# Merge gates of the tail in pairs by seven block products instead of eight

## The chip, the cores and the metric

The kernel runs on one core of a Trainium2 chip. The metric is device time in microseconds of one execution. The core's engines are named as in the profile: PE (matmuls), DVE, ACT and POOL (element-wise work), SP (issues the DMAs).

## The reference, cut to what matters

Two layers; in each, a combined projection of h = RMSNorm(x) gives the inputs of four branches A, B, C, M and the logits of four merge gates. Sequence length and model width are both 1024.

```python
h = rms_norm(x, norm_g)
z = h @ w_in                                   # a_u, a_v, a_gate, ..., merge_logits (4 x 1024 columns)
y_a = chunked_spatial_gating(gelu(a_u), gelu(a_v), ...) * silu(a_gate)
y_b, y_c, y_m = ...                            # attention, state space layer, memory attention
gates = sigmoid(merge_logits + b_merge).reshape(bsz, seq, 4, 1024)
merged = sum(gates[:, :, i] * (y_i @ w_br_i) for i in range(4))
x = x + merged @ w_out
```

The merge logits alone are a product of 1024 x 1024 by 1024 x 4096 in each layer.

## The kernel before, in words

Activations lie transposed: channels on the 128 partitions, 1024 tokens along the free dimension. x times its norm gain stands in eight tiles `xg[0..7]`, one for each 128 input channels. Every fp32 product is made of three matmuls: each operand is split into a rounded high part and the rest (`xh`, `xl`; `wh`, `wl`), and hi·hi, hi·lo and lo·hi are summed in PSUM (`mmr`, L176). The rest is one subtraction: by DVE, or by POOL when `split` or `wsplit` is told so (both under `tt`, L96). A cast of raw weights is DVE's (L152).

A block of 128 output channels (`cm`) is 48 matmuls of 512 columns: 8 input tiles x 3 products x 2 token halves. `cmn` adds the row scale: one DVE operation that reads PSUM and multiplies by `rsb`. A merge gate is such a block, then a tanh with the bias on ACT. There are 32 gates in a layer, index (i, c): branch i, 128-channel block c.

In each layer the work around the change runs in this order:

1. Attention, with fillers in the gaps of PE's queue (`background`): the silu gate blocks of branches B, C, M, whose results go to DRAM (`ysscr`), and 10 of the 32 merge gates (the list `BG`: all eight of i = 1, and (3, 6), (3, 7)), written to DRAM (`bgscr`).
2. `branch_a`: two products `av` (96 matmuls of 256 columns each), each followed by a chain on DVE, ACT and POOL (gelu, norm, split); then four blocks au0, ag0, au1, ag1 of 48 matmuls, each evicted from PSUM by DVE; then the spatial product (`pv`, 4 times 3 matmuls), transposes (`tr`) and the split results `yah`, `yal`.
3. `merge` for i = 0, 2, 3, 1. For each c: the gate, computed in place (48 matmuls, DVE, ACT) or fetched from `bgscr`; the product y_i @ w_br_i (12 matmuls, 24 for i = 1); the eviction `stt` on DVE, which multiplies by the gate; and an addition into `merged` (on POOL, on DVE for the last i). 22 gates of a layer are computed in place. `gated` fetches the split inputs of the next merge from `ysscr`, in the midst of the merge before it (`AH`).
4. Eight blocks of the output product and the residual.

The PSUM pool for blocks (`mm`) holds two tiles of 128 x 1024: the block after next has to wait for an eviction. A scheduler sets the order on each engine's queue from priorities in program order; each engine then takes its queue strictly in that order.

Of the kernel before, what the change touches and what calls it, by code (L numbers as in the profile page):

```python
# [44 lines left out]
class Trunk:  # L45
# [174 lines left out]
    def setup(self):  # L220
# [45 lines left out]
        self.bgscr = self.dp.tile([len(BG), P, S], F32, name="bgscr")  # L266
# [984 lines left out]
    def background(self, l, bi, bias=None, y=None, ri=None, dst=None):  # L1251
# [4 lines left out]
        low = lambda: self.tc.high_priority(offset=-LOW)  # L1256
        with self.tc.high_priority(offset=-800):
            hi, lo = self.wsplit(self.a["w_cm"][l, bi], 1024, bg=True)
# [66 lines left out]
    def branch_a(self, l):  # L1325
# [7 lines left out]
        for tg in range(2):  # L1333
            ps = self.mm()
            for j in range(4):
# [71 lines left out]
    def merge(self, l, i, ys, first=False, last=False, ahead=None):  # L1407
# [8 lines left out]
        res = None  # L1416
# [7 lines left out]
        for c in range(8):  # L1424
            if ahead and ahead[0] == c:
                res = ahead[1]()
# [23 lines left out]
        return res  # L1450

    def run(self):
# [17 lines left out]
        for l in range(self.L):  # L1470
# [72 lines left out]
AH = (6, 4, 3)  # L1543
# [123 lines left out]
```

## Time and profile before

| | us |
|---|---|
| median of 3 runs | 2438.87 (2436.58 to 2439.66) |
| the profiled execution, its own time | 2440.25 |
| its span in the profile | 2438.5 |
| PE busy | 2325.2 (95%) |
| DVE busy | 1215.9 (50%) |
| POOL busy | 775.0 (32%) |
| ACT busy | 706.5 (29%) |

Busy is the time in which an engine had an instruction in it, its waiting inside one included. Layer 1's branch A runs from 720.7 to 789.4 us, its merges from there to 1132 and its output product to 1236; in layer 2 branch A runs from 1920.5 to 1989.6 and the merges to 2332.

### The profile page before, as it was taken

To read this page: it belongs to the slowest core of one execution; us is meant where nothing else is said; L and a number is where in the kernel's file an instruction comes from. 1 tells how busy PE (TensorE), PEld (TensorE's weight loads), DVE (VectorE), ACT (ScalarE), POOL (GpSimd) and SP (SyncE) were. 2 spreads that over 40 slices of the span, in tenths; PEclk is the share of its full clock that TensorE was granted. 3 is DMA by queue.
4 is the path that set the end of the run, shared out by engine and by line. 5 is a ranking of instruction groups with operands and counts; after the bars stand their busy time and mean duration, and the time that the engine had idled before them with its cause. 6 is when DMAs were issued, how large, how long until landed. Compare 5 with 4: busy or idle time off the path is not lost. (4 is left out here: it accounts for less than half of the span.)

```text
span 2438.5 us, 28178 instructions
## 1 busy us (share of the span) xinstructions
PE 2325.2 (95%) x11174; PEld 1855.2 (76%) x11174; DVE 1215.9 (50%) x1871; ACT 706.5 (29%) x1233; POOL 775.0 (32%) x605
## 2 busy tenths in 40 slices
PE   7998889989999999999999888999999999999999
PEld 5766677867778888888877666787777888888887
DVE  6455784366676323236244556714666652233351
ACT  4121253247762101101111213522577420111010
POOL 3533113432304214342435421143322132244411
PEclk9999999999999999999999999999999999999999
DMA  4226343242332112222432363413423211122342
GB/s 153 75 93 184 115 138 102 82 123 79 95 106 66 61 44 70 69 77 105 156 100 73 96 188 108 139 49 103 125 83 109 80 44 52 56 92 79 103 156 69
DMA packets 91700, 237.56 MB, mean 97 GB/s; under 512 B 25200, under 2 KB 34352, under 8 KB 91568
## 3 DMA queue, kind: packets, MB, share of 16 engines
q1 hardware_dynamic: 91568, 235.76, 30.4%
q8 instruction: 88, 1.44, 0.2%
q14 instruction: 44, 0.36, 0.1%
HBM read 175.27 MB, written 60.46 MB: 97 GB/s over the span
## 5 line engine op out<-in xcount | busy, mean ns | idle before, releaser
L96 POOL TENSOR_TENSOR wl<-wr,wh 128x1024 fp32r<-128x1024 f32 (+3 forms) x125 | 295.9, 2367 | 946.1 <-DVE wh L152 634.7
L176 PE MATMUL mm<-xh,wh 128*128 128x512 f32 x1216 | 378.7, 392 | 9.1 <-ACT xh L106 8.7
L152 DVE CAST wh<-wr 128x1024 fp32r<-128x1024 f32 (+2 forms) x110 | 78.4, 713 | 618.6 <-PE mm L176 539.8
L176 PE MATMUL mm<-xh,wl 128*128 128x512 f32 x1216 | 376.1, 390 | 0.8 <-POOL wl L96 0.8
L176 PE MATMUL mm<-xl,wh 128*128 128x512 f32 x1216 | 376.8, 390 | 0.0
L176 PEld LDWEIGHTS mm<-xh,wh 128*128 128x128 f32 x1216 | 227.3, 188 | 59.9 <-ACT xh L106 8.7
L176 PEld LDWEIGHTS mm<-xh,wl 128*128 128x128 f32 x1216 | 228.3, 188 | 49.7 <-POOL wl L96 1.6
L176 PEld LDWEIGHTS mm<-xl,wh 128*128 128x128 f32 x1216 | 228.4, 188 | 49.0 <-issue 0.8
L176 PE MATMUL bg<-xh,bh 128*128 128x512 f32 x576 | 229.2, 416 | 15.5 <-DVE bgx L96 15.5
L176 PE MATMUL bg<-xl,bh 128*128 128x512 f32 x576 | 226.3, 411 | 0.0
L176 PE MATMUL bg<-xh,bl 128*128 128x512 f32 x576 | 224.1, 409 | 1.0 <-POOL bl L96 1.0
L96 POOL TENSOR_TENSOR bl<-br,bh 128x1024 fp32r<-128x1024 f32 x36 | 96.4, 2678 | 317.0 <-DVE bh L152 203.3
L106 ACT ACTIVATE cmn<-cmn,bmh 128x1024 f32<-128x1024 f32 x44 | 50.6, 1151 | 440.7 <-DVE cmn L96 440.7
L96 DVE TENSOR_TENSOR pT<-tr,pT 128x512 fp32r<-128x512 f32 x224 | 125.6, 571 | 42.8 <-ACT pT L106 42.1
L176 PEld LDWEIGHTS bg<-xh,bh 128*128 128x128 f32 x576 | 111.8, 195 | 46.0 <-DVE bgx L96 25.6
L176 PE MATMUL pv<-pT,v 128*128 128x512 f32 (+3 forms) x384 | 134.0, 388 | 7.9 <-DVE pT L96 5.1
L106 ACT ACTIVATE pT<-tr 128x512 fp32r<-128x512 f32 x224 | 111.0, 505 | 86.6 <-PE tr L1087 77.3
L176 PEld LDWEIGHTS bg<-xh,bl 128*128 128x128 f32 x576 | 111.1, 193 | 24.9 <-issue 3.2
L1054 DVE TENSOR_REDUCE mx<-mm 128x1 f32<-128x128 f32 (+7 forms) x128 | 96.5, 754 | 64.5 <-PE mm L176 63.7
L176 PEld LDWEIGHTS bg<-xl,bh 128*128 128x128 f32 x576 | 111.3, 194 | 21.8 <-issue 4.0
L106 ACT ACTIVATE pr<-mm,nm,qs 128x128 f32<-128x128 f32 (+7 forms) x128 | 106.3, 830 | 0.9
L1087 PE MATMUL tr<-ident,pr 128*128 128x128 f32 x576 | 97.9, 275 | 0.3 <-ACT pr L106 0.2
(449 smaller groups left out, 4173.7 us busy)
## 6 DMA issues: line engine op xcount, KB each, us to landing
wr<-in_w_cm_dram SPq DMA_DIRECT2D x76, 512.0 KB, 3.6
br<-in_w_cm_dram SPq DMA_DIRECT2D x36, 512.0 KB, 3.7
bgscr<-bgx SPq DMA_DIRECT2D x20, 512.0 KB, 3.1
gate<-bgscr SPq DMA_DIRECT2D x20, 512.0 KB, 5.6
ysscr<-bgx SPq DMA_DIRECT2D x16, 512.0 KB, 2.6
br<-ysscr SPq DMA_DIRECT2D x16, 512.0 KB, 3.4
wr<-in_w_out_dram SPq DMA_DIRECT2D x16, 512.0 KB, 3.7
bgr<-riscr SPq DMA_DIRECT2D x24, 256.0 KB, 4.8
```

The lines of the kernel that those rows point to most:

```text
L96: (eng or self.nc.vector).tensor_tensor(out=out, in0=x, in1=y, op=op)
L106: self.nc.scalar.activation(out, x, f, **k)
L152: self.nc.vector.tensor_copy(hi[:, :n], raw)
L176: self.nc.tensor.matmul(out, lhsT, rhs, start=start, stop=stop)
L1054: nc.vector.reduce_max(out=mx, in_=ps[:, 0:n], axis=AX.X)
L1087: nc.tensor.transpose(pt[:, k * P:(k + 1) * P], pts[k][:, st * P:(st + 1) * P], self.ident)
```

## The change

The 22 gates that were computed in the merges are computed ahead of them, as 11 pairs (c, c+1), and written to `bgscr` like the others; the merges fetch all 32.

A pair is a product of two 128-row weight blocks with x: seen as 2 x 2 blocks (output block by half of the input channels; half of the input channels by half of the tokens), it takes eight block products. Strassen's form (Winograd's variant) makes it of seven, with sums of the weight blocks and of the x blocks. A block product is 12 matmuls of 512 columns, so a pair is 84 matmuls instead of 96.

The sums of x are formed once in a layer from the split parts (`xh`, `xl`), for k = 0..3, and are split again: T3, T2 in `x_sums` (k = 0, 1 in program order behind the first av product's matmuls, k = 2, 3 behind the second's), T4 in `x_sums2` behind each au block, T1 in `x_sums3`, which overwrites the second token half of `xg[0..3]`. The weight sums are formed for each pair: four DVE additions and seven splits, each split a copy on ACT and a subtraction, two of them on DVE and five on POOL. A product's result is combined by DVE additions that read PSUM; the row scale becomes a POOL multiplication, then come tanh and DMA by halves of 512 columns.

```diff
+            for k in range(2):
+                self.x_sums(2 * tg + k)
...
+            for k in range(2):
+                self.x_sums2(2 * b + k)
...
+        self.x_sums3()
...
+    def x_sums(self, k):
...
+        self.tt(t3, h22, h12, SUB, eng=g)
+        self.tt(t2, l22, l12, SUB)
+        self.tt(t3, t3, t2, ADD)
+        self.split(*self.T[3][k], t3)
+        self.tt(t1, h12, h11, SUB, eng=g)
+        self.tt(t2, t3, h11, ADD)
+        self.tt(t2, t2, l11, ADD)
+        self.split(*self.T[2][k], t2)
+        self.tt(t3, l12, l11, SUB, eng=g)
+        self.tt(t1, t1, t3, ADD, eng=g)
+
+    def x_sums2(self, k):
...
+        self.tt(a, h21, h2, SUB, eng=self.nc.gpsimd)
+        self.tt(b, l21, l2, SUB)
+        self.tt(a, a, b, ADD)
+        self.split(*self.T[4][k], a)
+
+    def x_sums3(self):
+
+        for k in range(4):
+            self.split(*self.T[1][k], self.t1[k // 2][:, k % 2 * 512:k % 2 * 512 + 512])
+
+    def pair_weights(self, aps):
...
+        self.tt(s1, a21, a22, ADD)
+        self.tt(s2, s1, a11, SUB)
+        self.tt(s3, a11, a21, SUB)
+        self.tt(s4, a12, s2, SUB)
+        for i, a in enumerate((a11, s2, s3, a12, s1, a22, s4)):
+            w = self.U("sw", F32R)
+            hi, lo = half(w)
+            self.split(hi, lo, a, sub_eng=self.nc.vector if i in (1, 4) else self.nc.gpsimd)
+            yield hi, lo
...
+            def prod(ps, x):
+                hi, lo = ws[len(nws)]
+                for k in range(4):
+                    xh, xl = self.T[x][k]
+                    sl = slice(k * P, (k + 1) * P)
+                    self.mmr(ps, hi[:, sl], xh, k == 0, False)
+                    self.mmr(ps, hi[:, sl], xl, False, False)
+                    self.mmr(ps, lo[:, sl], xh, False, k == 3)
...
+            self.act(u1, prod(q1, 11), AF.Copy)
+            self.tt(u2, prod(q2, 2), u1, ADD)
+            q1, q2 = half(self.mm())
+            self.tt(u3, prod(q1, 3), u2, ADD)
+            finish(0, c1[0], prod(q2, 21), u1)
+            q1, q2 = half(self.mm())
+            p5 = prod(q1, 1)
+            self.tt(u4, p5, u2, ADD)
+            finish(1, c2[1], p5, u3)
+            finish(0, c2[0], prod(q2, 4), u3)
+            finish(1, c1[1], prod(self.pv(), 22), u4)
+            done(c1, c2)
...
+        def finish(h, out, x, y):
+            self.tt(out, x, y, ADD)
+            self.tt(out, out, self.rsb[:, h * 512:h * 512 + 512], MUL, eng=self.nc.gpsimd)
...
-            if (i, c) in BG:
-                g = self.U("gate")
-                nc.sync.dma_start(out=g, in_=self.bgscr[BG.index((i, c))])
-            else:
-                g = self.cmn(l, B_MRG + 8 * i + c)
-                self.act(g, g, AF.Tanh, scale=0.5, bias=self.bm_half[:, l * 32 + 8 * i + c:l * 32 + 8 * i + c + 1])
+            g = self.U("gate")
+            nc.sync.dma_start(out=g, in_=self.bgscr[8 * i + c])
...
-                self.tt(self.mg[c], self.mg[c], g, ADD, eng=None if last else nc.gpsimd)
+                self.tt(self.mg[c], self.mg[c], g, ADD, eng=nc.gpsimd if c % 2 and not last else None)
...
-            ys = self.merge(l, 0, ysa, first=True, ahead=(AH[0], lambda: self.gated(2, 2)))
-            ys = self.merge(l, 2, ys, ahead=(AH[1], lambda: self.gated(3, 0)))
-            ys = self.merge(l, 3, ys, ahead=(AH[2], lambda: self.gated(1, 4)))
-            self.merge(l, 1, ys, last=True)
+            self.gate_pairs(l, todo[::2], lambda: get(2, 0))
+            self.merge(l, 0, ysa, first=True, ahead={2: lambda: get(3, 0)})
+            self.merge(l, 2, ys[2], ahead={0: lambda: get(1, 4)})
+            self.merge(l, 3, ys[3])
+            self.merge(l, 1, ys[1], last=True)
```

Two smaller edits: the last filler gate of attention, (1, 3) of `bg_gate`, loses its low priority (`fore`), and `gated` takes its raw tiles from the general pool.

How the queues change is seen at three places of layer 1. The first is DVE at the second eviction of branch A, `av<-mm,rs` (the first av's chain ends with `av<-av,ry,ga x4`). Before:

```order
L103 SCALAR_TENSOR_TENSOR av_1279_6288<-av_1279_6288,ry_1283_6301,ga_1273_6185 128x256 x4
L96 TENSOR_TENSOR av_1287_6426<-mm_1286_6329,rs_63_381 128x1024
L100 TENSOR_SCALAR avt_1288_6427<-avt_1288_6427 128x1024
L96 TENSOR_TENSOR avt_1288_6427<-avt_1288_6427,av_1287_6426 128x1024
L103 SCALAR_TENSOR_TENSOR av_1287_6426<-avt_1288_6427,av_1287_6426 128x1024
```

After, with `tp` and `T` the tiles of the x sums:

```order
L103 SCALAR_TENSOR_TENSOR av_1291_6324<-av_1291_6324,ry_1295_6337,ga_1273_6185 128x256 x4
L96 TENSOR_TENSOR tp_1299_6462<-xl6_38_185,xl2_26_145 128x512
L96 TENSOR_TENSOR tp_1299_6462<-tp_1299_6462 128x512
L96 TENSOR_TENSOR tp_1300_6475<-xl7_41_195,xl3_29_155 128x512
L96 TENSOR_TENSOR tp_1299_6462<-tp_1299_6462,xh2_25_144 128x512
L96 TENSOR_TENSOR T_1286_6295<-tp_1299_6462,T_1284_6293 128x512
L96 TENSOR_TENSOR tp_1299_6462<-tp_1299_6462,xl2_26_145 128x512
L96 TENSOR_TENSOR tp_1300_6475<-tp_1300_6475 128x512
L96 TENSOR_TENSOR av_1301_6488<-mm_1298_6365,rs_63_381 128x1024
L96 TENSOR_TENSOR T_1282_6291<-tp_1299_6462,T_1280_6289 128x512
L96 TENSOR_TENSOR T_1286_6295<-tp_1300_6475,T_1284_6293 128x512
L96 TENSOR_TENSOR tp_1300_6475<-tp_1300_6475,xh3_28_154 128x512
```

Seven operations of `x_sums` now stand between the end of the first chain and that eviction, and more of them between the steps of the second chain behind it.

The second is PE at the end of branch A (`pv` the spatial product, `tr` its transposes, `mm_1341` the first merge gate before; `mm_1371` with weight `sw` the first product of the first pair after). Before:

```order
L176 MATMUL pv_1322_6727<-avh_1274_6187,wsr_1295_6470 128x512
L176 MATMUL pv_1322_6727<-avl_1276_6189,wsr_1295_6470 128x512
L176 MATMUL pv_1322_6727<-avh_1274_6187,wsr_1295_6470 128x512
L176 MATMUL mm_1341_6788<-xh2_25_144,wh_1339_6784 128x512 x2
L176 MATMUL mm_1341_6788<-xl2_26_145,wh_1339_6784 128x512 x2
L1400 MATMUL tr_1323_6732<-ident_43_204,sA_1320_6721 128x128 x4
L1400 MATMUL tr_1324_6738<-ident_43_204,sA_1320_6721 128x128 x4
```

After:

```order
L176 MATMUL pv_1351_6852<-avh_1275_6188,wsr_1309_6532 128x512
L1405 MATMUL tr_1352_6857<-ident_43_204,sA_1349_6846 128x128 x4
L1405 MATMUL tr_1353_6863<-ident_43_204,sA_1349_6846 128x128 x4
L176 MATMUL mm_1371_6908<-xh0_18_123,sw_1360_6883 128x512
L176 MATMUL mm_1371_6908<-xl0_19_124,sw_1360_6883 128x512
L176 MATMUL mm_1371_6908<-xh0_18_123,sw_1360_6883 128x512
L176 MATMUL mm_1371_6908<-xh1_22_134,sw_1360_6883 128x512
```

The spatial products and transposes no longer stand among the matmuls of a gate, but all ahead of the first pair's first product. On DVE the sums `sa` of the first pair's weights stand directly behind the last `yal` of branch A.

The third is DVE between the first merge (`merged7`) and the second (`cmn` before, `gate` after), with `wkh`, `wh` casts of weights and `bl`, `ys` the rests of the fetched inputs of the last merge. Before:

```order
L103 SCALAR_TENSOR_TENSOR merged7_1401_7381<-cmn_1395_7310,mm_1400_7368 128x1024
L152 CAST wkh_1403_7385<-wr_1402_7383 128x1024
L152 CAST wh_1422_7544<-wr_1421_7542 128x1024
L96 TENSOR_TENSOR cmn_1405_7389<-mm_1409_7396,rsb_89_557 128x1024
L103 SCALAR_TENSOR_TENSOR cmn_1405_7389<-cmn_1405_7389,mm_1410_7447 128x1024
L152 CAST wh_1428_7617<-wr_1427_7615 128x1024
L96 TENSOR_TENSOR cmn_1411_7462<-mm_1415_7469,rsb_89_557 128x1024
```

After:

```order
L103 SCALAR_TENSOR_TENSOR merged7_1606_8616<-gate_1604_8601,mm_1605_8603 128x1024
L152 CAST wkh_1608_8620<-wr_1607_8618 128x1024
L96 TENSOR_TENSOR bl_1611_8625<-yr_1612_8626,bh_1610_8624 128x1024
L96 TENSOR_TENSOR bl_1614_8631<-yr_1615_8632,bh_1613_8630 128x1024
L96 TENSOR_TENSOR ys_1617_8637<-yr_1618_8638,ys_1616_8636 128x1024
L96 TENSOR_TENSOR ys_1620_8643<-yr_1621_8644,ys_1619_8642 128x1024
L152 CAST wkh_1627_8684<-wr_1626_8682 128x1024
L103 SCALAR_TENSOR_TENSOR gate_1622_8648<-gate_1622_8648,mm_1623_8650 128x1024
L96 TENSOR_TENSOR merged0_1576_8479<-merged0_1576_8479,gate_1622_8648 128x1024
```

Before, a gate's matmuls on PE lay between two evictions of a merge, and the rests of fetched inputs stood among them one by one; after, the merge evictions follow each other, and four rests and two casts stand together ahead of the second merge's first.

## Rows read from the trace of the kernel before

**Rows 1.** The page, part 1: busy time of each engine, share of the span, instructions.

```profile
PE 2325.2 (95%) x11174; PEld 1855.2 (76%) x11174; DVE 1215.9 (50%) x1871; ACT 706.5 (29%) x1233; POOL 775.0 (32%) x605
```

**Rows 2.** Windows by hand: stretch, length, each engine's busy time, TensorE clock, DMA share.

```profile
core 0: us, PE busy (x) PEld busy (x) DVE busy (x) ACT busy (x) POOL busy (x), PEclk, DMA share, GB/s
700.00:720.00 20.00, 19.69 (x112) 15.16 (x111) 12.69 (x22) 12.38 (x27) 0.00 (x0) 1.00 0.07 27
720.70:789.40 68.70, 67.70 (x388) 59.55 (x388) 47.97 (x71) 16.88 (x22) 25.21 (x16) 1.00 0.31 98
789.40:1132.00 342.60, 342.22 (x1514) 282.05 (x1513) 116.97 (x107) 41.34 (x39) 116.70 (x49) 1.00 0.23 76
1920.50:1989.60 69.10, 69.10 (x395) 60.79 (x395) 40.24 (x68) 15.04 (x21) 24.80 (x16) 1.00 0.22 67
1989.60:2332.00 342.40, 341.04 (x1506) 279.98 (x1505) 121.20 (x109) 42.20 (x40) 118.06 (x48) 1.00 0.25 78
```

**Rows 3.** Waits of PE, 720 to 1130 us.

```profile
PE mm L176 <- DVE wkl L96: 1.0, 2, 0.5
PE mm L176 <- DVE gate L103: 0.3, 1, 0.3
```

**Rows 4.** Timeline of PE in layer 2's gates: start, duration, instruction, count.

```profile
2008.48 0.61 PE L176 MATMUL mm<-xh,wh 128*128 128x512 f32 x2
2008.93 0.62 PE L176 MATMUL mm<-xl,wh 128*128 128x512 f32 x2
```

**Rows 5.** Groups by form on DVE: shapes, count, busy us, mean ns, idle before.

```profile
L96 DVE TENSOR_TENSOR cmn<-mm,rsb 128x1024 f32<-128x1024 f32 x52 | 63.3, 1217 | 0.0
L103 DVE SCALAR_TENSOR_TENSOR gate<-gate,mm 128x1024 f32<-128x1024 f32 x20 | 24.4, 1218 | 17.0 <-PE mm L176 9.8 <-DMA gate<-bgscr 7.2
L96 DVE TENSOR_TENSOR sz<-sz,ph 128x512 f32<-128x512 f32 x16 | 10.2, 680 | 0.1
```

**Rows 6.** The same view on POOL.

```profile
L96 POOL TENSOR_TENSOR wl<-wr,wh 128x1024 fp32r<-128x1024 f32 x95 | 231.8, 2440 | 798.2 <-DVE wh L152 594.4 <-PE mm L176 188.6 <-DVE fi L96 12.0
L96 POOL TENSOR_TENSOR merged<-merged,cmn 128x1024 f32<-128x1024 f32 x28 | 67.9, 2427 | 33.1 <-DVE cmn L103 33.1
L96 POOL TENSOR_TENSOR st<-sd,sb 128x512 f32<-128x512 f32 x16 | 18.1, 1206 | 46.2 <-DVE stt L96 45.9
```

**Rows 7.** Timeline of DVE in layer 1's branch A.

```profile
728.88 2.79 DVE L103 SCALAR_TENSOR_TENSOR bgx<-bgx,bgy 128x1024 f32<-128x1024 f32 x1 [0.92 <-DMA bgy<-ybscr]
...
752.92 1.22 DVE L96 TENSOR_TENSOR av<-mm,rs 128x1024 f32<-128x1024 f32 x1
...
774.97 3.24 DVE L103 SCALAR_TENSOR_TENSOR sg<-sg,cmn 128x1024 f32<-128x1024 f32 x1 [1.13 <-ACT sg L106]
...
781.63 1.21 DVE L96 TENSOR_TENSOR cmn<-mm,rsb 128x1024 f32<-128x1024 f32 x1
```

**Rows 8.** Timeline of POOL in the same stretch.

```profile
728.19 2.40 POOL L96 TENSOR_TENSOR wl<-wr,wh 128x1024 fp32r<-128x1024 f32 x1 [46.66 <-DVE wh L152]
...
774.74 2.39 POOL L96 TENSOR_TENSOR wl<-wr,wh 128x1024 fp32r<-128x1024 f32 x1
777.09 1.72 POOL L96 TENSOR_TENSOR avl<-av,avh 128x256 fp32r<-128x256 f32 x1
...
781.84 2.41 POOL L96 TENSOR_TENSOR wl<-wr,wh 128x1024 fp32r<-128x1024 f32 x1 [0.68 <-DVE wh L152]
```

**Rows 9.** Timeline of PE at the end of layer 1's branch A.

```profile
789.59 0.39 PE L176 MATMUL pv<-avh,wsr 128*128 128x512 f32 x1
...
794.67 1.09 PE L1400 MATMUL tr<-ident,sA 128*128 128x128 f32 x8
```

**Rows 10.** Chain of waits around layer 2's last merge: start, us, what.

```profile
2324.75 4.61 DMA gate<-bgscr
```

**Rows 11.** DMA rate in 40 slices, 1100 to 1131 us, in layer 1's last merge.

```profile
GB/s 375 423 233 5 0 0 0 0 0 0 32 106 322 407 423 423 307 11 0 0 0 0 0 0 0 0 0 16 143 285 402 423 423 423 412 423 418 407 407 412
```

More of the change, by code (lines that the diff above doesn't have):

```diff
@@ L265, in setup @@
         self.ybscr = self.dp.tile([4, P, S], F32, name="ybscr")
-        self.bgscr = self.dp.tile([len(BG), P, S], F32, name="bgscr")
+        self.bgscr = self.dp.tile([32, P, S], F32, name="bgscr")
         self.ysscr = self.dp.tile([8, P, S], F32, name="ysscr")
@@ L1405, in branch_a @@
         return ya
-    def merge(self, l, i, ys, first=False, last=False, ahead=None):
+    def x_sums(self, k):
+        g = self.nc.gpsimd
+        if k == 0:
+            at = lambda t, j: [x[j // 2][:, j % 2 * 512:j % 2 * 512 + 512] for x in t]
+            half = lambda j, h: [x[:, h * 512:h * 512 + 512] for x in self.xg[j]]
+            b = lambda tag: self.bp.tile([P, 1024], F32R, tag=tag, name=self._n("T"), **({"bufs": 1} if tag == "br" else {}))
+            f = lambda: self.fp.tile([P, S], F32R, tag="ft", name=self._n("T"))
+            t2, t3 = ([b("bh"), b("bh")], [b("bl"), b("bl")]), ([f(), f()], [f(), b("br")])
+            self.T = {i: [at(t, j) for j in range(4)] for i, t in ((2, t2), (3, t3))}
+            for i, h in ((11, 0), (1, 1)):
+                self.T[i] = [half(j, h) for j in range(4)]
+            for i, h in ((21, 0), (22, 1)):
+                self.T[i] = [half(j + 4, h) for j in range(4)]
+            self.t1 = [self.U("t1") for _ in range(2)]
+        ap = lambda i: [x.bitcast(F32) for x in self.T[i][k]]
+        (h11, l11), (h12, l12), (h22, l22) = ap(11), ap(1), ap(22)
+        t = self.U("tp")
+        t3, t2 = t[:, 0:512], t[:, 512:1024]
+        t1 = self.t1[k // 2][:, k % 2 * 512:k % 2 * 512 + 512]
+        self.tt(t3, h22, h12, SUB, eng=g)
[8 more added lines that the diff above has]
+        self.tt(t1, t1, t3, ADD, eng=g)
@@ new lines, in pairs @@
+    def pairs(self, todo, late):
+        half = lambda t: (t[:, 0:512], t[:, 512:1024])
+        nxt = self.pair_weights(todo[0][0])
+        ws = [next(nxt) for _ in range(7)]
+        for n, (_, finish, done) in enumerate(todo):
+            nxt = self.pair_weights(todo[n + 1][0]) if n + 1 < len(todo) else None
+            nws = []
+            if not nxt:
+                late()
+            def prod(ps, x):
[6 more added lines that the diff above has]
+                    self.mmr(ps, lo[:, sl], xh, False, k == 3)
+                nws.append(next(nxt) if nxt else None)
+                return ps
+            (u1, u2), (u3, u4) = half(self.U("us")), half(self.U("us"))
+            c1, c2 = [half(t.bitcast(F32)) for t in self.wpair()]
+            q1, q2 = half(self.mm())
[4 more added lines that the diff above has]
+            finish(0, c1[0], prod(q2, 21), u1)
+            q1, q2 = half(self.mm())
+            p5 = prod(q1, 1)
[4 more added lines that the diff above has]
+            done(c1, c2)
+            ws = nws
@@ new lines, in gate_pairs, with done, f @@
+    def gate_pairs(self, l, pairs, late):
+        def finish(h, out, x, y):
+            self.tt(out, x, y, ADD)
+            self.tt(out, out, self.rsb[:, h * 512:h * 512 + 512], MUL, eng=self.nc.gpsimd)
+        def done(at):
+            def f(*cs):
+                for k, c in enumerate(cs):
+                    b = l * 32 + at + k
+                    for h in range(2):
+                        self.act(c[h], c[h], AF.Tanh, scale=0.5, bias=self.bm_half[:, b:b + 1])
+                        self.nc.sync.dma_start(out=self.bgscr[at + k][:, h * 512:h * 512 + 512], in_=c[h])
+            return f
+        self.pairs([([self.a["w_cm"][l, B_MRG + 8 * i + c + k] for k in range(2)], finish, done(8 * i + c)) for i, c in pairs], late)
@@ L1409, in merge @@
+    def merge(self, l, i, ys, first=False, last=False, ahead={}):
         nc = self.nc
@@ L1424, in merge @@
         for c in range(8):
-            if ahead and ahead[0] == c:
-                res = ahead[1]()
+            if c in ahead:
+                ahead[c]()
             if c % per == 0:
@@ L1542 @@
 NU = 38
-AH = (6, 4, 3)
 NBW = 2
```

30 lines of the change are left out of this document (22 added, 8 removed).

## The prediction

> **What bounds the kernel now.** I read the page's busy times first: PE is busy for 95% of the span, DVE for half of it [rows 1]. An average hides stages, so next came windows cut at branch A and the merges. In the merges of both layers PE has work in 342.2 of 342.6 and 341.0 of 342.4 us, and in branch A in 67.7 of 68.7 and 69.1 of 69.1, at the full clock [rows 2]. PE's waits in that stretch of layer 1 are 1.0 and 0.3 us [rows 3]. So the tail is bound by PE's count of matmuls alone, and a matmul less is time less, if nothing else comes late. What would come late is the question, because the other engines are hidden today: while PE works through a gate of 48 matmuls, DVE has one eviction to do and POOL one weight split and one addition.
>
> **What is saved.** Two 512-column matmuls start every 0.453 us [rows 4], so one costs 0.2267 us. A pair needs 84 instead of 96. 12 x 11 pairs x 2 layers = 264 matmuls x 0.2267 = **59.9 us**, 29.9 a layer, all on the path. The gates of all 32 indices now go through DRAM, which moves work between stages but adds no matmul. Making one filler gate urgent moves matmuls between attention and its end and is counted at nothing: PE has no gap there to speak of [rows 2] (700 to 720 us).
>
> **DVE and POOL don't run side by side.** This decides the price of all that is added. At 728.19 POOL starts a weight split of 2.40 us; DVE's operation on two SBUF tiles starts at 728.88 and takes 2.79 us, where its like take 1.22: it ends at 731.67, 1.08 after POOL. At 774.74 POOL splits for 2.39 us, DVE's `sg` starts at 774.97 and takes 3.24, and then POOL's next, an `avl` of 128x256, takes 1.72 instead of some 0.8 [rows 7, 8]. The waits add up as if only one of the two ran at a time. An eviction, which reads PSUM, is untouched: 1.21 us beside a POOL split of 2.41 [rows 7, 8]. So I count DVE operations with two SBUF inputs and POOL operations as one queue, the pair's time.
>
> The Trainium skill, "SBUF — State Buffer", section "Who interferes with whom", says the same and against this change: a VectorE instruction with two SBUF inputs and a GpSimd one that reads SBUF use one port pair, which the first to issue holds for its whole length. The trace agrees (3.24 us for `sg`). By that rule the sum is the one below; without it, it is the first rival's.
>
> **Branch A and the start of the pairs.** The x sums add, in a layer, 40 DVE operations of 128x512 and 20 on POOL (per k: 6 and 4 in `x_sums`, 3 and 1 in `x_sums2`, 1 and 0 in `x_sums3`). DVE's price is 0.68, POOL's 1.21 [rows 5, 6]: 27.2 + 24.2 = 51.4 us of the pair's time. ACT's 16 copies are off the path.
>
> Today's pair's time in branch A of layer 1: DVE 47.97 + POOL 25.21 = 73.2 [rows 2]. Of that some 7.5 us are evictions that read PSUM (five of 1.22, two half ones), and some 8 are waits inside operations, of the kind just shown (1.6, 2.0, 0.9 in the three of [rows 7, 8], the rest in others like them). That leaves 57 us. The first four POOL sums may run before, where POOL has nothing to do [rows 2] (700 to 720 us): -4.8. Before PE can start the second product of the first pair (the sum of T3), the end of branch A has to pass: `sg` 1.2, the product with it on POOL 2.4, two rests 2.4, two weight sums 1.4, two POOL rests 2.4, together 9.8. Sum: 57 + 51.4 - 4.8 + 9.8 = 113.4 us, so that product starts no earlier than 720.7 + 113.4 = 834.1. Without a stall it would start at 796.5: PE's own work ends at 789.4, then 12 spatial matmuls (2.7 us) and 16 transposes (1.7) [rows 9], which had a gate's matmuls among them before and stand alone now, and 2.7 us of the first product. Loss 37.6 us, if the pair is never idle. In layer 2 the same sum from 40.24 + 24.80 = 65.0 [rows 2], less 7 and some 5, is 53, so 109.4 after 1920.5: 2029.9 against 1989.6 + 7.1 = 1996.7, a loss of 33.2.
>
> Where PE will stand: the second `av` eviction, which now starts at 752.92 [rows 7], comes behind seven x sums, two of which need POOL sums that stand behind the first chain's `avl`. ag0 needs that eviction's PSUM tile, so PE waits in front of ag0; then in front of au1, whose weight cast stands behind the second chain, and in front of the first pair. The queues are fixed, so the pair will be idle for some of the time (ACT steps of about 1 us between DVE's). I add 4.5 a layer: 42 and 38, **80 us** for both. From below: 24 a layer (the first rival's), from above 55, with the pair idle for a sixth of the time.
>
> **The pairs.** PE needs 84 x 0.2267 = 19.0 us for one. The pair's time: four sums and two rests on DVE (4.1), five rests and four row scalings on POOL (10.9), 15 of 19. Seven additions from PSUM are beside it. That fits, and the weights are made one pair ahead. Bounds 0 and 8 us a layer; I take 3: **6 us**.
>
> **The merges.** Their gates' matmuls were the cover. In merges 0, 2 and 3, PE now needs 24 x 12 x 0.2267 = 65.3 us, 2.72 for each c. DVE has 24 evictions of 1.22 [rows 5], 8 additions of 1.22, 6 casts of 0.69 and 6 rests of 1.22, 51 us; the pair's time is 21 on DVE and 8 additions and 6 weight splits of 2.4 on POOL [rows 6], 34: 55 of 65. On the average it fits, but not in the second merge, where four rests and two casts, 6.3 us with POOL's splits among them, stand ahead of the first eviction, and PE has two PSUM tiles, 5.4 us. The gates are 24 x 0.5 MB, with weights and inputs 19 MB in 65 us, 290 GB/s. In the last merge of before, which already lives on gates from DRAM, the rate goes to 423 [rows 11], so it can be had, but in layer 2 the chain waits 4.61 us for one gate there [rows 10]. Bounds 4 and 25 a layer; I take 12: **24 us**. The last merge (24 matmuls for each c) and the output product stay as they are.
>
> **Sum.** 2438.5 - 59.9 + 80 + 6 + 24 = 2488.6 of span. The profiled execution's own time is 1.75 above its span and 1.4 above the median of the runs: 2488.6 + 1.75 - 1.4 = **2489**.
>
> **Rivals.**
> *DVE and POOL do run side by side.* Then DVE's own sum counts, 41 + 27 + 6 = 74 us, below the 75.8 until the second product, and what is left are stalls of order: some 8 in front of ag0, 5 of au1, 11 in front of the first pair, 24 a layer. With 2 for the pairs and 6 for the merges a layer: 2438.5 - 59.9 + 64 = 2442.6, so 2443, range 2425 to 2462. Against it: [rows 7, 8]. For it: a lock could bind less where both sides have short operations.
> *Faster.* The x sums fit beneath branch A, as POOL idles for 43 of its 69 us and DVE for 21 in layer 1 [rows 2], and the deep pool of tiles lets the merges run from fetched gates. Then 10 us a layer are lost: 2398.6, so 2399. The place is the second `av` eviction: if it comes before PE has finished au0, 10.9 us (48 matmuls) after av1's, so at the latest some 11 us later than its matmuls end, ag0 doesn't wait and this rival holds; each us beyond is lost. For it: the four POOL sums in an empty stretch. Against it: the 114 us of the pair's time against 76.
> *Worse.* Both unknowns at their upper ends: 55 a layer in branch A, 6 in the pairs, 22 in the merges: 2438.5 - 59.9 + 166 = 2544.6, so 2545. It decides where the fixed orders leave the pair idle for a sixth of branch A and the gates come at half of 423 GB/s.
>
> **Chances.** Forecast (2470 to 2530): 0.55. Side by side: 0.22. Faster: 0.13. Worse (2530 to 2565): 0.10. The range leaves out most of the faster rival and the upper part of the worse one: 2420 to 2550. A measurement can tell 0.2%, about 4.9 us, from no change. Faster by over that: all of the faster rival and a fourth of the side-by-side one, 0.19; same, 0.07; slower, 0.74.
>
> **What would show it.** In the profile after: PE's waits in branch A, none before, on the DVE evictions `av` and `cmn` and on the cast `wh`, and on the weights `sw`, together 35 to 45 us in each layer. DVE's two-input operations of 128x512 at a mean well above 0.69, POOL's above 1.21, while evictions stay at 1.22. In the pairs PE without gaps at 19.0 us each. In the merges waits on `gate` and on the evictions at the start of merge 2. The forecast is wrong if the new DVE operations take 0.69 beside a running POOL; if PE gets through branch A with less than 15 us of waits; or if the pairs take over 21 us each, in which case the loss lies in them and not ahead of them.

## The result, and the profile after

The changed kernel takes 2556.64 us (median of 4 runs, 2552.46 to 2558.91), the kernel before 2438.07 beside it: a ratio of 1.0488, 95% interval 1.0473 to 1.0503. It is slower by 118.6 us, where 50 were forecast, and lies just outside the range. The direction came true, and so did the size of the largest term; two others were too small by a factor of two and of nine.

The head of the page after and the busy times of the engines, which answer to [rows 1]:

```profile
span 2553.5 us, 28800 instructions
PE 2320.3 (91%) x10910; PEld 1825.6 (71%) x10910; DVE 1475.7 (58%) x2165; ACT 839.1 (33%) x1485; POOL 964.1 (38%) x783
```

PE has 264 matmuls less to do and is busy for about as long as before, in a span that is 115 us longer; DVE's busy time grows from 1215.9 to 1475.7 us and POOL's from 775.0 to 964.1.

Layer 1 of the changed kernel by windows (columns as in [rows 2]): from the first `av` eviction to the first pair's second product; the pairs; merge 0; merges 2 and 3; merge 1:

```profile
core 0: us, PE busy (x) PEld busy (x) DVE busy (x) ACT busy (x) POOL busy (x), PEclk, DMA share, GB/s
731.27:831.59 100.32, 72.58 (x313) 58.17 (x312) 81.15 (x103) 30.54 (x46) 56.15 (x35) 0.83 0.08 24
831.59:1065.52 233.93, 213.93 (x913) 168.59 (x912) 113.76 (x141) 79.22 (x127) 125.43 (x96) 1.00 0.32 108
1065.52:1101.90 36.38, 27.04 (x98) 20.64 (x96) 14.18 (x14) 7.82 (x8) 4.76 (x4) 0.86 0.58 217
1101.90:1155.23 53.33, 47.25 (x192) 36.52 (x193) 50.22 (x34) 0.00 (x0) 39.99 (x15) 0.97 0.65 239
1155.23:1198.75 43.52, 43.52 (x193) 36.05 (x192) 30.46 (x24) 6.41 (x7) 7.70 (x4) 1.00 0.31 118
```

PE's own matmuls would take 60.1 us in the first (the 53.2 from that eviction to the end of branch A in the kernel before, 4.4 and 2.7, less the overlap of 0.2), 206.7 in the second (11 x 19.04 - 2.7), 21.8, 43.5 and 43.5 in the last three. So 40.2, 27.2, 14.6 and 9.8 us are lost, and nothing in the last merge. PE is no longer full anywhere before that merge, and its clock is at 0.83 and 0.86 in two windows, where [rows 2] have 1.00 throughout.

The balance of the two profiled spans closes. The first `av` eviction is a poor mark for it, since it doesn't always meet PE at the same place: in layer 2 it comes 10.7 us ahead of au0's first matmul before the change and 4.2 us after it. So from here on A is the stretch from au0's first matmul (740.67 in layer 1) to the first pair's second product, 50.4 us of matmuls (192 x 0.2267, 4.4 and 2.7, less 0.2). P is the rest of the pairs, M from there to the first residual addition `xres`, 119.7 us of matmuls (24 x 2.72, 8 x 5.44, and one block of the output product):

| us | layer 1 | layer 2 |
|---|---|---|
| A: measured, PE's own, lost | 90.9, 50.4, 40.5 | 92.7, 50.4, 42.3 |
| P | 233.9, 206.7, 27.2 | 235.4, 206.7, 28.7 |
| M | 145.2, 119.7, 25.5 | 145.2, 119.7, 25.5 |
| saved matmuls | -29.9 | -29.9 |
| what the kernel before lost itself in the same stretch | -3.4 | -6.9 |
| sum | 59.9 | 59.7 |

The stretches ahead of A, which hold little of the change (the filler gate without its low priority, the first x sums), add -5.4 us in layer 1 and +0.8 in layer 2. Together 115.0 of 115.0. (The merges of the kernel before run to 1144.3 us in layer 1 and not to 1132, where the window of [rows 2] ends; the balance counts them whole.)

**A: taking turns.** DVE in the middle of branch A of layer 1, and below it POOL at the same time (start, duration, instruction):

```profile
753.76 1.75 DVE L96 TENSOR_TENSOR tp<-xl,xl 128x512 f32<-128x512 f32 x1
755.43 1.75 DVE L96 TENSOR_TENSOR tp<-tp,xh 128x512 f32<-128x512 f32 x1
757.10 1.74 DVE L96 TENSOR_TENSOR T<-tp,T 128x512 fp32r<-128x512 f32 x1
...
761.04 1.21 DVE L96 TENSOR_TENSOR av<-mm,rs 128x1024 f32<-128x1024 f32 x1
```

```profile
753.25 1.71 POOL L96 TENSOR_TENSOR t<-xh 128x512 f32<-128x512 f32 x1
754.93 1.70 POOL L96 TENSOR_TENSOR tp<-xh,xh 128x512 f32<-128x512 f32 x1
756.59 1.70 POOL L96 TENSOR_TENSOR t<-xh 128x512 f32<-128x512 f32 x1
...
760.65 1.60 POOL L96 TENSOR_TENSOR t<-t,tp 128x512 f32<-128x512 f32 x1
```

DVE's operations of 0.68 us take 1.75 in these rows, POOL's of 1.21 take 1.7, and they end one after the other, one of each every 1.67 us: nearly the sum of the two and far from the larger. The eviction at 761.04 reads PSUM and takes 1.21 beside a running POOL.

PE's waits in A, which were none in [rows 3]:

```profile
PE mm L176 <- DVE av L96: 10.6, 1, 10.6
PE pv L176 <- ACT sA L106: 7.6, 2, 6.4
PE mm L176 <- DVE ry L100: 2.7, 1, 2.7
PE mm L176 <- ACT sw L106: 2.5, 1, 2.5
PE mm L176 <- POOL wl L96: 2.2, 1, 2.2
PE tr L1405 <- ACT sA L106: 1.6, 2, 0.8
PE mm L176 <- POOL sw L96: 0.6, 1, 0.6
```

They are 27.8 of the 40.5 us lost; the rest is PE at a slower pace. The first is the second `av` eviction, 8 us later than at [rows 7] and behind the x sums. The second lies among the spatial products: ACT's copy `sA` (811.78) stands behind `sg`, and that waits for DVE's eviction of ag1 (809.50). The third and fifth are in front of and in au1, whose weight cast on DVE (777.51, 0.68 us) ends together with the operation `ry` that the view names. By the records of both engines, DVE and POOL stand idle together for 7.1 of the 100.3 us of the first window above. After the first wait PE's matmuls run at half speed for a while (a row is two matmuls; the last has the pace of [rows 4]):

```profile
762.31 1.22 PE L176 MATMUL mm<-xh,wh 128*128 128x512 f32 x2 [10.57 <-DVE av L96]
763.33 1.06 PE L176 MATMUL mm<-xl,wh 128*128 128x512 f32 x2
...
767.69 0.62 PE L176 MATMUL mm<-xl,wh 128*128 128x512 f32 x2
```

**P: a ring of four queues.** The end of one pair and the start of the next, on DVE, POOL, ACT and PE:

```profile
874.86 0.68 DVE L96 TENSOR_TENSOR wh<-pv,us 128x512 f32<-128x512 f32 x1
...
876.27 1.28 POOL L96 TENSOR_TENSOR wh<-wh,rsb 128x512 f32<-128x512 f32 x1
...
877.59 0.72 ACT L106 ACTIVATE wh<-wh,bmh 128x512 f32<-128x512 f32 x1 [0.52 <-POOL wh L96]
878.21 0.58 ACT L106 ACTIVATE us<-mm 128x512 f32<-128x512 f32 x1
...
878.85 4.83 PE L176 MATMUL mm<-T,sw 128*128 128x512 f32 x20 [1.64 <-ACT us L106]
...
900.14 1.19 PE L176 MATMUL mm<-T,sw 128*128 128x512 f32 x4 [1.67 <-ACT us L106]
```

DVE's last addition of a pair (874.86) stands behind the next weights' sums. POOL scales its result, ACT makes the tanh, and behind that in ACT's queue stands the copy `us<-mm` of the next pair's first product. PE waits 1.64 us for it after four matmuls of the second product, which goes to the other half of the same PSUM tile. That recurs in every pair: 878.85, 900.14, and so on, 21.29 us apart instead of 19.04. The remaining 0.6 us a round are three spells, one behind the wait and two behind no gap, in which the matmuls come at 0.23 to 0.34 instead of 0.2267 us. The first two periods are longer still, 25.1 and 22.2.

**M: gates behind weights.** SP's queue in merge 0, and DVE in the same stretch:

```profile
1068.69 0.32 SPq L1533 DMA_DIRECT2D bgscr<-wh  x1
...
1070.54 0.38 SPq L1561 DMA_DIRECT2D gate<-bgscr  x1
1081.85 0.33 SPq L149 DMA_DIRECT2D wr<-in_w_br_dram  x1
1082.28 2.52 SPq L1561 DMA_DIRECT2D gate<-bgscr  x5
```

```profile
1078.64 0.69 DVE L152 CAST wkh<-wr 128x1024 fp32r<-128x1024 f32 x1
1079.25 1.21 DVE L103 SCALAR_TENSOR_TENSOR merged<-gate,mm 128x1024 f32<-128x1024 f32 x1
1087.52 2.50 DVE L103 SCALAR_TENSOR_TENSOR merged<-gate,mm 128x1024 f32<-128x1024 f32 x2 [7.05 <-DMA gate<-bgscr]
```

After 1070.54 SP issues nothing for 11 us: its next entry is a weight load that waits for POOL to free the raw tile, and five gate fetches stand behind it. DVE then waits 7.05 us for a gate.

### The profile page after: what moved, and what is told of

Same layout as the page of the kernel before. It is cut to its first block, busy times and chain, and to the rows that moved or that the text cites. A ratio compares the mean times of both kernels' runs of the same rounds, so it can differ in the third digit from the quotient of the medians.

```text
span 2553.5 us, 28800 instructions
## 1 busy us (share of the span) xinstructions
PE 2320.3 (91%) x10910; PEld 1825.6 (71%) x10910; DVE 1475.7 (58%) x2165; ACT 839.1 (33%) x1485; POOL 964.1 (38%) x783
## 5 line engine op out<-in xcount | busy, mean ns | idle before, releaser
L96 POOL TENSOR_TENSOR wl<-wr,wh 128x1024 fp32r<-128x1024 f32 (+3 forms) x81 | 198.9, 2457 | 507.5 <-DVE wh L152 243.0
L176 PE MATMUL mm<-T,sw 128*128 128x512 f32 x792 | 197.2, 398 | 36.1 <-ACT us L106 30.9
L176 PEld LDWEIGHTS mm<-T,sw 128*128 128x128 f32 x792 | 146.8, 190 | 80.2 <-ACT us L106 39.4
L176 PE MATMUL mm<-xh,wh 128*128 128x512 f32 x512 | 165.4, 403 | 37.7 <-DVE av L96 23.2
L176 PE MATMUL mm<-xh,sw 128*128 128x512 f32 x528 | 177.5, 403 | 8.7 <-ACT sw L106 4.9
L176 PE MATMUL mm<-xh,wl 128*128 128x512 f32 x512 | 162.7, 399 | 5.1 <-POOL wl L96 5.1
L176 PE MATMUL mm<-xl,wh 128*128 128x512 f32 x512 | 163.4, 400 | 0.0
L176 PEld LDWEIGHTS bg<-xh,bh 128*128 128x128 f32 x576 | 111.0, 193 | 46.3 <-DVE bgx L96 25.9
L176 PEld LDWEIGHTS mm<-xh,wh 128*128 128x128 f32 x512 | 97.2, 193 | 62.9 <-DVE av L96 24.0
L176 PEld LDWEIGHTS mm<-xh,sw 128*128 128x128 f32 x528 | 101.0, 192 | 38.8 <-DVE us L96 9.4
L96 POOL TENSOR_TENSOR sw<-wr,sw 128x512 fp32r<-128x512 f32 x66 | 93.6, 1421 | 85.1 <-ACT sw L106 48.1
```

The costliest lines, as they stand in the source:

```text
L96: (eng or self.nc.vector).tensor_tensor(out=out, in0=x, in1=y, op=op)
L176: self.nc.tensor.matmul(out, lhsT, rhs, start=start, stop=stop)
```

## The experiments

Each is an edit of the changed kernel. The table has A, P, M as above for layers 1 and 2, and F, the stretch from layer 1's last residual addition to au0's first matmul in layer 2 (before 714.2). Each row is one profiled execution. Executions of one kernel differ by up to 11 us (e15: 2574.11 and 2585.25), and stages that an edit leaves alone differ too: F from 709.7 to 715.0, with the operations of DVE, ACT and POOL in one and the same order in most of these runs; A from 90.3 to 94.3, and to 96.8 in e11; P from 233.9 to 238.3; M from 143.3 to 145.5. A single edit is therefore read by its stage rather than by its total, and a stage that stays inside these ranges counts as unchanged.

| run | median | A | P | M | F |
|---|---|---|---|---|---|
| the change | 2556.6 | 90.9, 92.7 | 233.9, 235.4 | 145.2, 145.2 | 715.0 |
| e1 | 2543.8 | 86.2, 87.3 | 235.5, 235.8 | 143.3, 144.7 | 710.7 |
| e3 | 2527.2 | 94.3, 91.7 | 224.4, 223.5 | 145.5, 143.8 | 709.7 |
| e5 | 2574.1 | 92.5, 92.9 | 236.8, 235.1 | 152.0, 150.8 | 713.1 |
| e6 | 2552.1 | 90.6, 92.1 | 234.9, 233.9 | 143.8, 144.9 | 710.9 |
| e7 | 2573.4 | 91.1, 92.2 | 238.3, 234.0 | 153.2, 152.1 | 712.7 |
| e8 | 2531.6 | 86.3, 89.1 | 225.7, 223.6 | 147.9, 145.6 | 713.1 |
| e9 | 2545.3 | 88.5, 88.8 | 236.6, 236.0 | 143.8, 143.6 | 713.5 |
| e10 | 2552.9 | 88.2, 88.9 | 237.5, 235.0 | 144.2, 144.7 | 715.0 |
| e11 | 2562.6 | 92.4, 96.8 | 235.6, 235.3 | 144.0, 143.3 | 713.5 |
| e12 | 2528.0 | 86.4, 88.9 | 226.5, 224.7 | 145.1, 145.6 | 713.2 |
| e13 | 2543.9 | 91.9, 93.1 | 235.2, 236.9 | 139.5, 138.4 | 712.0 |
| e14 | 2574.8 | 92.4, 91.6 | 235.2, 235.2 | 153.1, 152.7 | 710.8 |
| e15 | 2579.7 | 91.9, 90.3 | 234.9, 235.3 | 153.9, 158.2 | 712.2 |

### Branch A: e1, e9, e2, e10

**e1**, the x sums on DVE alone:

```diff
-        g = self.nc.gpsimd
+        g = self.nc.vector
...
-        self.tt(a, h21, h2, SUB, eng=self.nc.gpsimd)
+        self.tt(a, h21, h2, SUB)
```

> The 20 operations of the x sums that POOL does in a layer are done by DVE instead. If DVE and POOL take turns (the lock of the prediction), 24.2 us of the pair's time become 13.6, and the stretch from the first av eviction to the first pair's second product, 100.3 us in layer 1 of the changed kernel, gets shorter by 5 to 10: about 2540 in all. If they run side by side, DVE carries 13.6 us more in that stretch and it grows: about 2575.

A fell by 4.7 and 5.4 us (from the first eviction, as the expectation counts, by 7.9 and 3.7). From that eviction in layer 1 (columns as above) DVE is now busy for 79.97 of 92.43 us, against 81.15 of 100.32 before the edit, with 16 more operations in the window: its waits inside operations went with POOL's work.

```profile
734.85:827.28 92.43, 67.19 (x286) 53.56 (x285) 79.97 (x119) 30.98 (x47) 41.90 (x19) 0.83 0.08 26
```

That speaks for taking turns, and against two engines side by side.

**e9**, the sums for k = 2, 3 behind the second `av` chain:

```diff
-            for k in range(2):
-                self.x_sums(2 * tg + k)
+            if tg == 0:
+                for k in range(2):
+                    self.x_sums(k)
...
+        for k in range(2, 4):
+            self.x_sums(k)
         ws = self.U("ws")
```

> The x sums for k = 2, 3 come behind the whole chain of the second av product in program order, so its eviction, on which PE waits 10.6 us in the changed kernel, no longer stands behind them. If the common time of DVE and POOL is what fills branch A, that wait falls below 2 us but comes back later, and the stretch from the first av eviction to the first pair's second product stays at 96 to 100 us: 2549 to 2560. If the order of the queue was the cause, the 10 us stay saved in each layer: about 2537.

PE's waits in layer 1's A:

```profile
PE mm L176 <- DVE rt L96: 16.9, 1, 16.9
...
PE mm L176 <- DVE av L96: 0.2, 1, 0.2
```

The wait on the eviction is gone, and one of 16.9 us in front of au1 stands in its place (the view names the small operation `rt`; the cast of au1's weights on DVE, 780.31, ends together with it). A fell by only 2.4 and 3.9: the order decides where PE waits, and the common time of DVE and POOL decides most of how long.

**e2**, no x sums:

```diff
-                self.x_sums2(2 * b + k)
...
-        self.x_sums3()
...
+            self.T[2], self.T[3], self.T[4] = self.T[11], self.T[22], self.T[21]
```

> Leaves the x sums out: the products of the pairs read halves of x itself, in the same number and size, so the gates are not those of the reference. If the sums are what fills branch A, that stretch falls from 100.3 us to about 70 (60.1 without any loss, plus the 10 us at its end that a gate covered before): about 2495. If the sums cost little and the loss is the order at the end of branch A, it stays above 85: about 2530. What is left against the kernel before lies in the pairs and the merges.

2493.6 us. From au0's first matmul to the first pair's first product it takes 58.8 and 60.4 us, against 84.6 and 86.4 with the sums and 47.7 of PE's own. So the sums cost 25.8 and 26.0 us a layer in place, out of 51.4 of common time, and 11.1 and 12.7 are lost without any sum, all of it behind the first spatial product, where no gate's matmuls stand any more.

**e10**, matmuls that nobody reads in the gaps at the end of branch A:

```diff
+                if g2 == 1 and b == 0:
+                    self.idle(28)
+                if g2 == 1 and b == 1:
+                    self.idle(6)
...
```

> Adds 34 matmuls a layer whose result nobody reads, at the end of branch A, where PE waits 6.4 us between the first two spatial products and about 1 us twice behind them. If the clock that falls to 1.2 GHz after such waits (0.68 granted in that stretch) costs time of its own, the spatial products, transposes and the first pair's first product run at full speed with the gaps filled, and 3 to 5 us a layer are won by more work: about 2549. If these operations are paced by DVE, ACT and POOL anyway, the time stays within 4 us of 2557 or grows by up to 7 us a layer where the filling comes too late to be done in time: up to 2570.

The spatial product behind the first gap, first in the change (one matmul, 0.79 us, 6.39 us of waiting before it), then with the gap filled (0.50 us):

```profile
812.50 0.79 PE L176 MATMUL pv<-avh,wsr 128*128 128x512 f32 x1 [6.39 <-ACT sA L106]
```

```profile
809.08 6.28 PE L176 MATMUL bg<-xh 128*128 128x512 f32 x27
815.62 0.50 PE L176 MATMUL pv<-avh,wsr 128*128 128x512 f32 x1 [0.27 <-ACT sA L106]
```

From the first spatial product to the second product of the first pair it took 23.8 and 24.9 us instead of 26.3 and 25.9, where PE's own are 6.9. In the other runs that leave this stretch alone it took 25.7 to 28.4. All of A fell by 2.7 and 3.8. So the slow clock was real there and cost some 1 to 4 us a layer; most of that stretch is paced by the other engines. The median fell by 3.8 us, which the spread of the runs doesn't tell from nothing. The stretches of slow clock behind the waits of 10.57 and 2.16 us were not filled in any run.

### The pairs: e3

```diff
-            self.act(u1, prod(q1, 11), AF.Copy)
+            self.ts(u1, prod(q1, 11), 1.0, MUL)
```

> The copy of each pair's first product out of PSUM is DVE's instead of ACT's. Theory: in ACT's queue it stands behind the tanh of the pair before, which waits for POOL's scaling, which waits for DVE's last addition; so PE's wait of 1.6 us in each of 10 pairs a layer goes, the pairs come every 19.0 to 19.6 us instead of 21.3: about 2520. Rival: PE then waits as long for the next thing, a weight split or another addition, and the time stays within 6 us of 2557.

The same copy in three pairs running, now on DVE:

```profile
944.05 0.69 DVE L100 TENSOR_SCALAR us<-mm 128x512 f32<-128x512 f32 x1 [0.91 <-PE mm L176]
...
963.61 0.69 DVE L100 TENSOR_SCALAR us<-mm 128x512 f32<-128x512 f32 x1 [0.78 <-PE mm L176]
...
983.09 0.69 DVE L100 TENSOR_SCALAR us<-mm 128x512 f32<-128x512 f32 x1 [0.77 <-PE mm L176]
```

The pairs come every 19.5 us, and P fell by 9.5 and 11.9 us. That settles the wait on ACT. The 19.5 against 19.04 are the slow spells, which here have no wait before them. The median fell by 29 us; of the 23.6 by which the profiled span is shorter, P made 21.4, and the rest lies in stages that the edit leaves alone.

### The merges: e4, e5, e7, e6, e13, e11, e14, e15

**e4**, plain gates of 96 matmuls a pair, ahead of the merges through DRAM, no x sums:

```diff
-            for k in range(2):
-                self.x_sums(2 * tg + k)
...
-            self.gate_pairs(l, todo[::2], lambda: get(2, 0))
+            for i, c in todo:
...
+                g = self.cmn(l, B_MRG + 8 * i + c)
+                self.act(g, g, AF.Tanh, scale=0.5, bias=self.bm_half[:, at:at + 1])
+                nc.sync.dma_start(out=self.bgscr[8 * i + c], in_=g)
```

> No products in seven and no x sums: the 22 gates are computed as before with 96 matmuls a pair, but ahead of the merges and through DRAM, and the merges are the changed ones. It prices the bare merges alone. If a merge without a gate's matmuls is short of DVE, POOL and gates by itself, merges 0, 2 and 3 take about 90 us a layer here too against 65 of PE's matmuls: about 2485. If only the pairs' late weights and tiles starve the merges, they take under 72 and the kernel is at 2438 to 2450.

2481.5 us, M 142.0 and 143.7: the merges lose 22 to 24 us a layer whatever computes the gates, once no gate's matmuls stand between their evictions.

**e5**, gate fetches issued by ACT, and **e7**, only one gate fetched in each merge:

```diff
-            nc.sync.dma_start(out=g, in_=self.bgscr[8 * i + c])
+            nc.scalar.dma_start(out=g, in_=self.bgscr[8 * i + c])
```

```diff
-            g = self.U("gate")
-            nc.sync.dma_start(out=g, in_=self.bgscr[8 * i + c])
+            if c == 0:
+                g1 = self.U("gate")
+                nc.sync.dma_start(out=g1, in_=self.bgscr[8 * i + c])
+            g = g1 if first else self.U("gated")
...
-                self.stt(g, g, 1.0, psy, ADD, MUL)
+                self.stt(g, g1, 1.0, psy, ADD, MUL)
```

> The merges' gate fetches are issued by ACT, idle there, instead of SP. Theory: in merge 0 DVE waits 3.3 and 7.1 us for gates because SP's queue holds their fetches behind a weight load that waits for POOL to free its raw tile; then these waits and the slow clock after them go, 8 to 12 us a layer: about 2537. Rival: the memory gives the gates no sooner, the waits stay and the time is within 6 us of 2557.

> Leaves out the fetches of the merges' gates but the first of each merge, which serves for all eight c, so the result is not the reference's. It takes 28 of 32 fetches of 512 KB out of the merges. If the gates' transfers are what the merges lack, the 25 us a layer of loss go nearly all: about 2507. If it is only the order on SP's queue in merge 0, it gains what the issue from ACT's queue gains, 8 to 12 a layer: about 2537, and the rest stays with DVE and POOL.

Both expectations failed. Windows of e5's merge 0 and of its merges 2 and 3 in layer 1:

```profile
1075.73:1106.88 31.15, 25.18 (x97) 19.61 (x96) 14.27 (x14) 7.82 (x8) 4.75 (x4) 0.89 0.77 289
1106.88:1169.30 62.42, 53.21 (x193) 41.36 (x193) 46.19 (x34) 0.00 (x0) 39.19 (x15) 0.84 0.53 193
```

Merge 0 gained what the theory said, 36.4 to 31.2 (e7: 28.3). But merges 2 and 3 grew from 53.3 to 62.4 (e7: 65.4), with one fetch for each merge in e7. So the gates' transfers are not what those two merges lack. What e5 lacks there shows in DVE's waits in the second window; the change has none on weights there:

```profile
DVE wh L152 <- DMA wr<-in_w_out_dram: 6.3, 2, 3.7
DVE wkh L152 <- DMA br<-in_w_br_dram: 4.8, 1, 4.8
```

These are casts of weights for the output product and the last merge. They stand in DVE's queue ahead of evictions of merges 2 and 3, and their loads come late: 11.1 us, and 9.5 in layer 2. In e7 DVE waits 1.3 us so, and PE waits 9.0 us for casts and splits of weights, against 4.1 in the change.

**e6**, all merge additions on DVE, and **e13**, no additions in merges 2 and 3:

```diff
-                self.tt(self.mg[c], self.mg[c], g, ADD, eng=nc.gpsimd if c % 2 and not last else None)
+                self.tt(self.mg[c], self.mg[c], g, ADD, eng=None)
```

```diff
-                self.tt(self.mg[c], self.mg[c], g, ADD, eng=nc.gpsimd if c % 2 and not last else None)
+                if last:
+                    self.tt(self.mg[c], self.mg[c], g, ADD)
```

> The eight additions a layer of merges 2 and 3 that POOL does (2.4 us each) are DVE's (1.22). DVE is busy for 52.9 of 56 us there. If DVE and POOL take turns, 9.6 us a layer of their common time go and the stretch gets 5 to 9 us shorter: about 2543. If they run side by side, DVE gets 9.8 us more than it has room for and the kernel is slower by 7 us a layer: about 2570.

> Leaves out the additions of merges 2 and 3 into the sum, so the result is not the reference's. It takes 9.8 us a layer off DVE, 19 off POOL, nothing off PE. If DVE's queue fills merges 2 and 3 (busy 50.2 of 53.3 us in layer 1), that stretch falls to PE's 43.5 to 46: about 2541 in all. If PE's short waits elsewhere and the slow clock make the loss, it stays above 50: about 2553.

Merges 2 and 3 of layer 1, e6 and then e13, and PE's waits there in e13:

```profile
1100.69:1154.62 53.93, 48.10 (x193) 37.22 (x194) 50.94 (x41) 0.00 (x0) 22.57 (x8) 0.94 0.70 260
```

```profile
1102.54:1150.65 48.11, 45.65 (x192) 37.02 (x193) 30.51 (x26) 0.00 (x0) 19.98 (x8) 0.96 0.78 295
```

```profile
PE mm L176 <- POOL wkl L96: 2.1, 1, 2.1
PE mm L176 <- DVE wkh L152: 2.0, 1, 2.0
```

In e6 POOL's 40.0 us became 22.6 and the stretch stayed at 53.9: what DVE no longer waits for POOL it works itself, busy for 50.9 us as for 50.2 before. Neither of the two expectations of e6 came true. Without the additions (e13) DVE is busy for 30.5 us and the stretch takes 48.1, in both layers; merge 3 alone takes 21.8, which is PE's own. So about 5 of the 10 us lost there are the additions, on whichever engine; the others lie in merge 2, at whose start its weights' cast and split stand behind the four rests (2.0 and 2.1 us of waits in e13 too, and the slow clock behind them).

**e11**, weights a merge ahead:

```diff
+            if c == 2 and i in (0, 2):
+                self.wq += [weights(j, {0: 2, 2: 3}[i]) for j in (0, 4)]
...
```

> Both weight blocks of merges 0, 2 and 3 are loaded and split a merge ahead, not two outputs ahead. If PE's waits on the casts and splits of these weights, 4.1 us, with the slow clock after them, are a loss of their own, and SP's queue with the gates behind the weight load another, 5 to 10 us a layer go: about 2542. If the merges lack DVE and POOL altogether, the waits move to the evictions and the time stays within 5 us of 2557.

M fell by 1.2 and 1.9 us, which is inside the range. The two waits on cast and split are gone, but two on evictions, 2.8 and 3.5 us in both layers, have come in their place, and merges 2 and 3 take 54.9 and 53.7 us. The weights' order was not the cause by itself.

**e14**, two matmuls that nobody reads behind each product of merges 2 and 3, and **e15**, the same on e5:

```diff
+            if i in (2, 3):
+                self.idle(2, wbr[0], ys[0][0])
...
```

> Adds two matmuls that nobody reads behind each product of merges 2 and 3, 7.3 us of PE's time a layer. If DVE's queue fills that stretch, PE's gaps take them in and merges 2 and 3 stay at 53 to 54 us: within 4 of 2557. If the slow clock makes the loss, the filled gaps keep it up, and the stretch falls below 52: about 2550. If PE itself has no gaps to spare it grows by 7 us a layer: about 2571.

> The same filling with the gate fetches issued by ACT, where merges 2 and 3 took 62.4 us with a granted clock of 0.84, against 53.3 at 0.97. If that clock is why the earlier gates brought no gain, the filled stretch comes down to 53 to 56 us: about 2558. If it is not, it stays at 61 to 70: 2574 to 2590.

In e14 merges 2 and 3 took 62.2 and 61.8 us, 8 to 9 more, for 7.3 of matmuls added. 14 of the 32 stood in one piece, in no gap, so this says little about gaps. In e15 they took 65.6 and 68.1, at a granted clock of 0.97 in layer 1 where e5 has 0.84. Since the same filling cost 8 to 9 us by itself in e14, this doesn't settle how much of e5's 62.4 and 61.2 the low clock made.

### Together: e8 and e12

e8 is e1, e3, e5 and e6 at once, e12 the same without e5.

> Four edits at once: x sums all on DVE, first product copied by DVE, gates fetched from ACT's queue, merge additions all on DVE. If they mend separate losses, the gains add up: 13 and 29 us measured, some 20 and 14 expected, about 2480, still slower than the kernel before. If they mend one and the same wait, no more than the largest is left: about 2525.

> Three edits that each gained alone: x sums on DVE (13 us), first product copied by DVE (29 us), merge additions on DVE (5 us). If they mend separate losses the gains add up: about 2510. With the gate fetches moved to ACT's queue as well it was 2532; the difference is then what that fourth edit costs.

2531.6 and 2528.0, above the sums of the gains (2480 and 2510). A and P keep what e1 and e3 gained; M keeps nothing. No run was as fast as the kernel before; the nearest, e4, has nothing of Strassen's products left in it and is still 43 us slower. A form that computes the pairs between the merges' products, which would give both their cover back, was not run. Whether its tiles (x's 16, the sums of x, seven weight sums, the merged sums) fit beside each other is not shown.

## Why the prediction was wrong, step by step

- **Saved: right.** PE's work fell by 264 matmuls, at the same pace outside of the slow spells; twenty of them take 4.83 us at 878.85, where 20 x 0.2267 is 4.53 and the rest is the last one's end and a slower first one.
- **DVE and POOL take turns: right** for operations on two SBUF tiles, by the rows at 753 to 758, by e1 and by e9. The rule of the Trainium skill ("SBUF — State Buffer", "Who interferes with whom") holds here, with 1.67 us for one of each.
- **Branch A: the size right, the make-up only in part**, 42 and 38 us forecast, 40.5 and 42.3 measured. The waits on the second `av` eviction, in front of au1 and on the first pair's weights are the ones named; the second largest, 7.6 us on `sA` in ACT's queue, is not, and all waits make 27.8 and 29.5 us where 35 to 45 were expected. The rest is a slower pace, which the sum didn't hold. By e2 the x sums cost 26 us, where the sum laid its whole loss on the common time of DVE and POOL, and 11 to 13 us are lost at the end of branch A with no x sum at all, where the sum had 9.8 us of common time and no loss without the sums. So that the size came true is in part luck.
- **Pairs: wrong, 3 us against 27.2 and 28.7**, and the upper bound of 8 with it. The step that failed is "that fits": it set 15 us of common work against 19.0 of PE. Capacity was there, but the order was not looked at. The first product's copy stands behind the last pair's tanh in ACT's queue, and that behind POOL and DVE. e3 took 9.5 and 11.9 us of it away by moving one copy. The rest is in the main the first two periods, where the second pair's weights come late (DVE waits 6.76 us for them at 838.77), and the slow spells. The prediction's own sign came, pairs of over 21 us; but more was lost ahead of them.
- **Merges: half, 12 us against 25.5.** The step that failed is the average over merges 0, 2 and 3, "55 of 65". Merge 0 has little work for DVE and loses 14.6 us, of which e5 gives back 5.2 by another order of the fetches and e7 8.1 without most of them; merges 2 and 3 hold the additions and the rests, DVE is busy for 50.2 of 53.3 us there, and they lose 9.8. The sum also left out work: it counts six weight splits on POOL in three merges, where merges 2 and 3 alone hold eight, since the weights of the last merge and of the output product are split there too. The rate of the gates limited merges 2 and 3 little: DVE waits 1.4 and 1.2 us for gates there in the two layers of the change.
- **Not in the sum:** -4.6 us ahead of branch A, and 10.3 us that the kernel before lost itself in these stretches, which the forecast left in both.

Of the rivals, the worse one (2545) came nearest, but not by its own mechanism: branch A stayed near the forecast, with DVE and POOL idle together for a fourteenth of it and not a sixth, and the pairs, to which it gave 6 us a layer, lost 28. Its 22 us for the merges were near.

Left open: why merges 2 and 3 grow by 9 to 12 us when the gates come earlier (e5, e7). In e5 the late loads of the next weights show as DVE's waits, 11.1 us; why they come later there, and the slow clock's part, was not isolated. Open too is what the slow spells in the pairs are.

## What to carry to other kernels

Before taking matmuls out of a stage that PE fills, list what these matmuls hide, and cost each queue's order there as well as its sum: a stage with 4 us of slack in 19 can still lose 2 in every round, if a short copy stands behind a long chain of other engines. Follow the ring of one round, from PE's last product through every queue back to its next wait. An average over stages is no bound where their loads differ, and one transfer in front of a queue can hold all that stand behind it.

## What the runs showed of the hardware that was not expected

- DVE operations of 0.68 us and POOL operations of 1.21 us on 128x512 tiles in SBUF, both queues full, alternate: one of each every 1.67 us, a little under the sum of 1.89.
- After waits of 10.57, 3.22 and 3.67 us, and after one of 2.16 shortly behind one of 2.74, PE's matmuls ran at 0.43 us each (1.2 GHz) before they came back to 0.2267 (2.4 GHz). The granted clock of whole windows fell to 0.83, and to 0.68 between 805 and 832 us.
- Matmuls that nobody reads kept that clock up in e10 (0.98 granted from 805 to 829 us, where the change has 0.68 from 805 to 832) and made the stretch from the first spatial product to the first pair's second product 2.5 and 1.0 us shorter.
